# Two rows of a feed-forward input copied within SBUF and transposed as rounded 32-bit, and a final norm whose sum of squares goes straight into the power

## The chip, the cores and the metric

The kernel runs on one core of one Trainium2 chip. The core has five engines that work side by side and wait for each other by semaphores: TensorE (PE, with its weight loads listed as PEld), VectorE (DVE), ScalarE (ACT), GpSimd (POOL) and SyncE (SP), which here only issues transfers (DMAs). Data live in SBUF (128 partitions) and matmul results in PSUM. The metric is the device time of one execution in microseconds. Three executions before the change took 1324.27, 1325.01 and 1326.56 us; their median, 1325.01, is the time before.

## The reference

One decoder block on a sequence of 1024 tokens with a model width of 1024, in 32-bit floating point. What matters here is its second half and the last norm:

```python
def rmsnorm(x, g):
    xf = x.astype(jnp.float32)
    xf = xf * lax.rsqrt(jnp.mean(xf * xf, axis=-1, keepdims=True) + EPS)
    return (xf * g.astype(jnp.float32)).astype(x.dtype)

h = rmsnorm(x, mix_norm_g[l])
...
x = x + y @ w_out[l]
h = rmsnorm(x, ffn_norm_g[l])
x = x + (jax.nn.silu(h @ w_gate[l]) * (h @ w_up[l])) @ w_down[l]
...
return rmsnorm(x, final_norm_g)
```

Ahead of it two attention mixers (a sliding window with sinks and a latent one) are computed from `h`, gated and summed to `y`.

## The kernel before, in words

The 1024 tokens are worked on as eight blocks of 128 rows. Every product of two 32-bit matrices is made of three matmuls (`mm3`, L172 to L174): each operand is split into a rounded part and a remainder (`split`, L163 on ACT and L166 on DVE), in a rounded 32-bit type ("fp32r" in the profile), and high by high, high by low and low by high are added in PSUM. The large products (output projection, gate and up, down) are done as a 2 x 2 block product with seven instead of eight block products, numbered q = 1 to 7; the sums of blocks that this needs are formed on DVE and POOL.

**The way into the feed-forward part.** While the last products of the output projection (`xo`, PSUM tiles `xo`) end, each block b of the residual `x2[b]` goes through these steps. `norm_a(b)` squares it on ACT with a running sum (L1742) and forms the reciprocal root on POOL (`rstd_of`, L361 and L364). `norm_b(b)` multiplies it on DVE by that root and by the gain, into the tile `xn` (L1747), and sends the residual to DRAM (L1748, `x_d<-x` in the profile). `to_h_of(b)` calls `to_h(xn, b)`: eight transposes of 128 x 128 on PE by an identity matrix (L1583), four into each of two PSUM tiles `tp`, which ACT and DVE then take out. For b = 0 to 3 they are split at once. For b = 4 to 7 the block sums with block b − 4 are formed too (tiles `t`, `hraw`, then `t2h`, `t2l`, `t3h`, `t3l`, `b22h`, `b22l`); the second part of this, `rest()` (L1611 and the two lines after), is called later as `lowers.pop(b)()`. From there the feed-forward products run as `ffn.run()`, PSUM tiles `fa` and `fb`.

**What sets the order.** Here the order on PE, DVE, ACT and POOL is that of the program text (`manual_schedule` on these four); SP's queue is ordered by the scheduler, except where `keep_in_program_order` pins a transfer. An engine works its queue strictly in order, so a wait holds back all that is behind it. SBUF tiles come from two shared pools of slots, `U` (21 slots) and `V` (17). A tile gets the slot of one that is finished, and its first writer waits for the last users of that one. One tile more changes which slots the next ones get.

**The end.** The down projection runs q by q over eleven pairs of tiles (`lr`, split to `lrv`; PSUM tiles `fd`). `down_done(q, t)` is called for each of four row tiles t when a product is complete; it adds the product to the residual quarter `xq[(i, d)]` (i the half of the rows, d the half of the columns) and squares that quarter on ACT with a running sum into `fin_s` (`sumsq`, L1931). For the first quarter of a row the sum is scaled and the gain multiplied in at once (`first_half`, L1948 and L1950); for the second quarter `final` (L1936 to L1943) adds the two sums, raises to the power −1/2 on POOL, and scales both quarters, one on DVE and one on ACT, which are sent out. In the last product, q = 3, the last five pairs are done row tile by row tile, so that three of the four row tiles are finished beside matmuls.

Of the kernel before, what the change touches and what calls it, by code (L numbers as in the profile page):

```python
# [8 lines left out]
F32 = mybir.dt.float32  # L9
F32R = mybir.dt.float32r  # L10
BF16 = mybir.dt.bfloat16
AF = mybir.ActivationFunctionType
ALU = mybir.AluOpType
# [4 lines left out]
P = 128  # L18
S = 1024
D = 1024  # L20
NB = S // P
NK = D // P
EPS = 1e-6
# [66 lines left out]
def hybrid_block_kernel(  # L90
# [29 lines left out]
    nc = tc.nc  # L120
# [19 lines left out]
    def uid(name):  # L140
        counter[0] += 1
        return f"{name}_{counter[0]}"

    def U(name, dt=F32, shape=(P, 1024)):
        return pool.tile(list(shape), dt, tag="u", name=uid(name))

    def V(name, dt=F32, shape=(P, 4, 512)):
        return vpool.tile(list(shape), dt, tag="v", name=uid(name))

    def tiny(name, w=1):  # L150
        return small.tile([P, w], F32, tag=f"t{w}", name=uid(name))

    def P1(name, shape=(P, 512), dt=F32):
        return ps1.tile(list(shape), dt, tag="ps", name=uid(name))

    def PX(name, shape=(P, 512), dt=F32):
        return psum["x"].tile(list(shape), dt, tag="ps", name=uid(name))
# [18 lines left out]
    def sub(out, a, b, eng):  # L176
        eng.tensor_tensor(out, a, b, op=ALU.subtract)  # L177

    def add(out, a, b, eng):
        eng.tensor_tensor(out, a, b, op=ALU.add)  # L180

    def blk(b, n=1):
        return slice(b * P, (b + n) * P)

    def half(s):
        return slice(512 * s, 512 * s + 512)


    ident_r = const.tile([P, P], F32R, name="ident_r")
    ident = ident_r.bitcast(F32)  # L190
# [168 lines left out]
    def rstd_of(ss, width, r=None):  # L359
        ms = tiny("ms")  # L360
        nc.gpsimd.tensor_scalar(ms, ss, 1.0 / width, EPS, op0=ALU.mult, op1=ALU.add)  # L361
        if r is None:
            r = tiny("rstd")
        nc.gpsimd.tensor_tensor(r, ms, neg_half, op=ALU.pow)  # L364
        return r

    def bcast_gain(name, g, w=1024):
        t = U(name)
        nc.sync.dma_start(t[:, 0:w], g.partition_broadcast(P))
        return t  # L370
# [57 lines left out]
    for g in range(NG):  # L428
        t = V("khd", F32R, (P, 2, S))
# [141 lines left out]
    ps = kvq_ps[0] = PX("kvq")  # L571
# [122 lines left out]
    def new_h(name):  # L694
        hq[name] = (V(name + "h", F32R), V(name + "l", F32R))

    def split_h(name, c, src, eng=None):
        hi, lo = hq[name]
        split(hi[:, :, blk(c)], lo[:, :, blk(c)], src, eng)
# [60 lines left out]
    ORDER = (1, 6, 2, 7, 5, 4, 3)  # L760
# [155 lines left out]
    for b in range(NB):  # L916
# [4 lines left out]
        ps = PX("ql", (P, 416))  # L921
# [12 lines left out]
        t = U("lat", F32, (P, C_CKV))  # L934
# [102 lines left out]
    for i, b in enumerate((4, 5, 6, 7, 0, 1, 2, 3)):  # L1037
        ps = P1("kl", (P, KVL))
        mm3(ps, [(hT(k, blk(b)), (wkl[k // 4][0][:, k % 4], wkl[k // 4][1][:, k % 4])) for k in range(NK)])
        t = U("lat", F32, (P, 2, KVL))  # L1040
# [3 lines left out]
        r = rstd_of(ss, KVL)  # L1044
# [531 lines left out]
    def to_h(xn, b):  # L1576

        c = b % 4
        pss = []
        for kh in range(2):  # L1580
            ps = (P1 if b < 5 else PX)("tp", (P, 4, P))
            for j in range(4):
                nc.tensor.transpose(ps[:, j], xn[:, blk(4 * kh + j)], ident)  # L1583
            pss.append(ps)
        if b < 4:
            if b == 0:
                new_h("b11")
                new_h("b21")
            raw1[b] = U("hraw", F32, (P, 2, 4, P))
            for kh in range(2):  # L1590
                nc.scalar.copy(raw1[b][:, kh], pss[kh])
                split_h(("b11", "b21")[kh], c, pss[kh])
            return
        if b == 4:
            for name in ("b22", "t2", "t3"):
                new_h(name)
        r = raw1.pop(c)
        t23 = U("t23", F32, (P, 2, 4, P))
        nc.scalar.copy(t23[:, 1], pss[0])
        sub(r[:, 0], pss[0], r[:, 0], nc.vector)  # L1600
        b22, t2, t3 = ([t[:, :, blk(c)] for t in hq[name]] for name in ("b22", "t2", "t3"))
        nc.scalar.copy(b22[0], pss[1])
        sub(t23[:, 0], pss[1], r[:, 0], nc.vector)
        nc.scalar.copy(t2[0], t23[:, 0])
        sub(t23[:, 1], pss[1], t23[:, 1], nc.vector)
        sub(b22[1], pss[1], b22[0].bitcast(F32), nc.vector)
        sub(r[:, 1], r[:, 1], t23[:, 0], nc.gpsimd)
        late.append((c, r))

        def rest():  # L1610
            nc.scalar.copy(t3[0], t23[:, 1])  # L1611
            sub(t2[1], t23[:, 0], t2[0].bitcast(F32), nc.vector)
            sub(t3[1], t23[:, 1], t3[0].bitcast(F32), nc.vector)

        return rest
# [103 lines left out]
    normed = {}  # L1719
# [16 lines left out]

    wop = {}

    def norm_a(b):
        xn = U("xn")  # L1740
        ss = tiny("ss")
        nc.scalar.activation(xn, x2[b], AF.Square, accum_out=ss)  # L1742
        normed[b] = xn, rstd_of(ss, D)

    def norm_b(b):
        xn, rs = normed[b]
        nc.vector.scalar_tensor_tensor(xn, x2[b], rs, fg_bc, op0=ALU.mult, op1=ALU.mult)  # L1747
        nc.sync.dma_start(x2_d[b], x2.pop(b))  # L1748

    def to_h_of(b):  # L1750
# [67 lines left out]
    xo(3, 0)  # L1818
    conv(7, 1)
    norm_a(0)  # L1820
    ahead(4, 1)
    ffn.load_part(0, 1)
    xo(6, 2)
    conv(4, 0)
    norm_b(0)
    xo(3, 1)
    conv(4, 1)
    norm_a(1)
    mix_of("g")
    nc.scalar.activation(tiny("si"), neg_half, AF.Silu)  # L1830
    xo(6, 3)
    norm_b(1)
    to_h_of(0)
    xo(3, 2)
    norm_a(2)
    mix_of("u")
    ffn.prep_to(2)
    xo(7, 0)
    norm_b(2)
    to_h_of(1)  # L1840
    xo(3, 3)
# [62 lines left out]
    while ffn.n_run < len(ffn.seq):  # L1904
        j, q, m = ffn.run()
# [13 lines left out]
    xq = {}  # L1919
# [4 lines left out]

    p1, u2, u3 = V("dp1"), V("du2"), V("du3")
    fing = bcast_gain("fing", fin_g)
    fin_s = const.tile([P, 2, 2, 4], F32, name="fin_s")

    def sumsq(i, d, t):
        junk = U("sq", F32, (P, 512))  # L1930
        nc.scalar.activation(junk, xq[(i, d)][:, t], AF.Square, accum_out=fin_s[:, i, d, t:t + 1])  # L1931

    def final(i, t, d):

        fs = fin_s[:, i, d, t:t + 1]
        nc.gpsimd.tensor_scalar(fs, fs, 1.0 / D, fin_s[:, i, 1 - d, t:t + 1], op0=ALU.mult, op1=ALU.add)  # L1936
        nc.gpsimd.tensor_tensor(fs, fs, neg_half, op=ALU.pow)
        y = xq[(i, d)][:, t]
        nc.vector.scalar_tensor_tensor(y, y, fs, fing[:, half(d)], op0=ALU.mult, op1=ALU.mult)
        nc.sync.dma_start(out[blk(4 * i + t), half(d)], y)  # L1940
        y = xq[(i, 1 - d)][:, t]
        nc.scalar.mul(y, y, fs)
        nc.scalar.dma_start(out[blk(4 * i + t), half(1 - d)], y)  # L1943

    def first_half(i, t, d):

        fs = fin_s[:, i, d, t:t + 1]
        nc.gpsimd.tensor_scalar(fs, fs, 1.0 / D, EPS, op0=ALU.mult, op1=ALU.add)  # L1948
        y = xq[(i, d)][:, t]
        nc.gpsimd.tensor_tensor(y, y, fing[:, half(d)], op=ALU.mult)  # L1950

# [2 lines left out]
    def down_done(q, t):  # L1954
        ps = banks["A" if q in (1, 2, 5, 3) else "B"][t]
        if q == 1:
            nc.scalar.copy(p1[:, t], ps)
        elif q == 6:
            add(u2[:, t], ps, p1[:, t], nc.vector)
            add(u2[:, t], u2[:, t], xq[(0, 1)][:, t], nc.gpsimd)  # L1960
        elif q == 7:
            add(u3[:, t], ps, p1[:, t], nc.vector)
            add(u3[:, t], u3[:, t], xq[(1, 1)][:, t], nc.gpsimd)
            add(p1[:, t], p1[:, t], xq[(1, 0)][:, t], nc.gpsimd)
        else:
            i, d = {2: (0, 0), 5: (1, 1), 4: (1, 0), 3: (0, 1)}[q]
            x_ = xq[(i, d)][:, t]
            add(x_, ps, {2: x_, 5: u3[:, t], 4: p1[:, t], 3: u2[:, t]}[q], nc.vector)
            sumsq(i, d, t)
            if q in (4, 3):  # L1970
                final(i, t, d)
            else:
                first_half(i, t, d)

    i = 0
    for q in ORDER:
# [12 lines left out]
        if not last_q:  # L1989
            for j in range(HF):  # L1990
                down_ahead(i)
                if i in (8, 14, 20, 26):
                    load_x2(*((0, 1), (0, 0), (1, 1), (1, 0))[(i - 8) // 6])
                for t in range(4):
                    step(j, t)
                lr.pop((q, j))
                i += 1
            for t in range(4):
                down_done(q, t)
        else:  # L2000
            for j in range(HF - LAST):
                down_ahead(i, HF, CONVS + 1)
                for t in range(4):
                    step(j, t)
                i += 1
            down_ahead(i, HF, HF)
            for t in range(4):
                for j in range(HF - LAST, HF):
                    step(j, t)
                down_done(q, t)  # L2010
# [90 lines left out]
```

## Time and profile before

| what | value |
|---|---|
| median of three runs | 1325.01 us (1324.27 to 1326.56) |
| profiled execution: its own time | 1323.36 us |
| profiled execution: its span, first to last instruction | 1320.8 us |
| TensorE busy in the span | 1308.5 us (99%) |
| VectorE busy | 916.1 us (69%) |
| ScalarE busy | 635.7 us (48%) |
| GpSimd busy | 560.8 us (42%) |
| granted TensorE clock, mean | 0.998 of full |
| moved by DMA | 245.12 MB |

The span is 2.6 us shorter than the execution's own time. A row of the timeline gives start and length in microseconds, the engine, the line of the kernel, the operation, output and inputs by the program's names, the shape, and in brackets how long the engine sat idle before it and what ended that. Matmuls overlap: one of 512 columns is listed with 0.39 us, but they start 0.23 us apart. "SPq" is SP's queue: the time shown there is that of issuing a transfer, not of its landing. A row of a stage gives the stage's bounds and length, the busy time of PE, PEld, DVE, ACT and POOL, the granted clock, the share of the DMA engines and GB/s.

### The profile page before, as it was taken

What the parts mean: (1) busy time and instruction counts of PE and PEld (TensorE: products, weight loads), DVE (VectorE), ACT (ScalarE), POOL (GpSimd) and SP (SyncE); (2) the same over time, 40 slices, a digit from 0 to 9 for tenths busy, and PEclk for the clock granted to TensorE, in tenths of its full rate; (3) what the DMA queues carried; (4) which work ended last, traced back from release to release, by engine and by line L of the source; (5) the groups of instructions that cost most, each with busy time, mean ns of one, the idle gap of its engine ahead of it and who ended that gap; (6) DMA issues with size and microseconds to landing.
All of it is one profiled execution on the core that took longest, in us unless ns stands there. A gap on an engine that the chain in (4) does not pass through costs nothing.

```text
span 1320.8 us, 19066 instructions
## 1 busy us (share of the span) xinstructions
PE 1308.5 (99%) x6516; PEld 1102.8 (83%) x6516; DVE 916.1 (69%) x1509; ACT 635.7 (48%) x1289; POOL 560.8 (42%) x623
## 2 busy tenths in 40 slices
PE   9999999999999999999999999999999999999997
PEld 6899888888888888888888888888888888888886
DVE  7868687786767777877779655756666554663962
ACT  7434667675456666654455232332223323644452
POOL 2115546552325556312232465777567631022521
PEclk9999999999999999999999999999999999999999
DMA  9454444456576478898521334655554435996503
GB/s 375 161 187 160 133 161 138 154 177 215 164 250 181 104 216 192 266 306 199 185 112 48 124 135 162 233 201 197 184 183 148 147 120 197 373 375 226 175 20 140
DMA packets 92192, 245.12 MB, mean 186 GB/s; under 512 B 10304, under 2 KB 17984, under 8 KB 90944
## 3 DMA queue, kind: packets, MB, share of 16 engines
q1 hardware_dynamic: 87264, 233.15, 51.0%
q0 software_dynamic: 3392, 8.39, 3.6%
q10 hardware_dynamic: 1440, 2.36, 0.5%
q8 instruction: 52, 0.85, 0.3%
q14 instruction: 44, 0.36, 0.1%
HBM read 161.16 MB, written 78.51 MB: 181 GB/s over the span
## 4 chain that ended last, share of the span: by engine, by line
PE 60%; POOL 2%; issue 2%; DVE 2%; ACT 1%; DMA 0%; POOLq 0%; DVEq 0%; SPq 0%; ACTq 0%
PE fa L172 6%; PE fa L174 6%; PE fa L173 6%; PE fd L173 5%; PE fd L174 5%; PE fd L172 5%; PE fb L173 5%; PE fb L174 5%; PE fb L172 5%; PE xo L174 2%; PE xo L173 2%; PE xo L172 2%; POOL p L1266 1%; POOL denb L1265 1%; PE oB L174 1%
## 5 line engine op out<-in xcount | busy, mean ns | idle before, releaser
L166 DVE TENSOR_TENSOR wl<-wr,wl 128x512 fp32r<-128x512 f32 x150 | 144.3, 986 | 74.0 <-ACT wl L163 73.5
L166 DVE TENSOR_TENSOR lrv<-lr,lrv 128x1024 fp32r<-128x1024 f32 x77 | 105.2, 1397 | 49.4 <-ACT lrv L163 43.4
L163 ACT CAST lrv<-lr 128x1024 fp32r<-128x1024 f32 x77 | 80.1, 1052 | 94.1 <-PE fd L174 52.2
L172 PE MATMUL fd<-lrv 128*128 128x512 f32 x308 | 119.8, 389 | 0.0
L173 PE MATMUL fd<-lrv 128*128 128x512 f32 x308 | 119.8, 389 | 0.0
L174 PE MATMUL fd<-lrv 128*128 128x512 f32 x308 | 119.8, 389 | 0.0
L177 POOL TENSOR_TENSOR wr<-wr,sm 128x512 f32<-128x512 f32 (+1 forms) x38 | 45.6, 1209 | 137.9 <-DVE wl L166 119.6
L163 ACT CAST wl<-wr 128x512 fp32r<-128x512 f32 x150 | 86.5, 621 | 3.8 <-DVE t3l L177 2.8
L166 DVE TENSOR_TENSOR wl<-sm,wl 128x512 fp32r<-128x512 f32 x60 | 50.3, 862 | 42.8 <-ACT wl L163 42.6
L1265 POOL TENSOR_TENSOR denb<-denb,neg_one 128x1 f32<-128x1 f32 x64 | 39.9, 623 | 92.6 <-ACT p L1264 80.7
L172 PEld LDWEIGHTS fd<-lrv 128*128 128x128 f32 x308 | 57.8, 188 | 12.1
L173 PEld LDWEIGHTS fd<-lrv 128*128 128x128 f32 x308 | 57.8, 188 | 12.0
L174 PEld LDWEIGHTS fd<-lrv 128*128 128x128 f32 x308 | 57.8, 188 | 11.9
L1264 ACT ACTIVATE p<-scb,nmb 128x384 f32<-128x384 f32 (+3 forms) x64 | 47.7, 746 | 32.0 <-DVE nmb L1263 24.9
L361 POOL TENSOR_SCALAR ms<-ss 128x1 f32<-128x1 f32 x32 | 8.6, 269 | 122.8 <-ACT xn L1742 45.5
L1263 DVE CUSTOM_DVE_ANT_0 scb<-scb,mask 128x384 f32<-128x384 f32 (+3 forms) x64 | 48.4, 761 | 17.4 <-PE scb L1255 16.4
L1638 ACT ACTIVATE act<-sm 128x512 f32<-128x512 f32 x11 | 7.0, 633 | 102.2 <-DVE sm L180 102.2
L166 DVE TENSOR_TENSOR ptl<-pTb,pth 128x512 fp32r<-128x512 f32 (+2 forms) x96 | 50.0, 550 | 8.0 <-ACT pth L163 7.8
L163 ACT CAST pth<-pTb 128x512 fp32r<-128x512 f32 (+2 forms) x96 | 43.4, 480 | 18.2 <-PE pTb L1280 17.2
L1266 POOL TENSOR_SCALAR p<-p,denb 128x384 f32<-128x384 f32 (+3 forms) x64 | 48.4, 756 | 6.3
L1638 ACT ACTIVATE act<-pu 128x512 f32<-128x512 f32 x22 | 13.9, 632 | 69.7 <-DVE pu L180 69.7
L172 PE MATMUL fa<-t1h,wl 128*128 128x512 f32 x120 | 47.1, 392 | 0.1
(354 smaller groups left out, 4291.0 us busy)
## 6 DMA issues: line engine op xcount, KB each, us to landing
lr<-la_d SPq DMA_DIRECT2D x77, 256.0 KB, 5.3
wr<-in_w_gate_dram SPq DMA_DIRECT2D x22, 512.0 KB, 4.4
wr<-in_w_up_dram SPq DMA_DIRECT2D x22, 512.0 KB, 5.1
la_d<-sd SPq DMA_DIRECT2D x22, 512.0 KB, 4.9
wd<-in_w_down_dram SPq DMA_DIRECT2D x22, 512.0 KB, 7.0
rb_d<-wd SPq DMA_DIRECT2D x22, 512.0 KB, 2.7
lr<-rb_d SPq DMA_DIRECT2D x44, 256.0 KB, 5.4
lr<-in_w_down_dram SPq DMA_DIRECT2D x33, 256.0 KB, 5.3
```

Source lines behind the costliest of these rows:

```text
L163: i = nc.scalar.copy(hi, src)
L166: (eng or nc.vector).tensor_tensor(lo, src, hi.bitcast(F32), op=ALU.subtract)
L172: nc.tensor.matmul(ps, ah, bh, start=first and i == 0, stop=False, skip_group_check=go_on)
L173: nc.tensor.matmul(ps, ah, bl, start=False, stop=False, skip_group_check=go_on)
L174: nc.tensor.matmul(ps, al, bh, start=False, stop=last and i == n - 1, skip_group_check=go_on)
L177: eng.tensor_tensor(out, a, b, op=ALU.subtract)
L361: nc.gpsimd.tensor_scalar(ms, ss, 1.0 / width, EPS, op0=ALU.mult, op1=ALU.add)
L1263: nc.vector.tensor_tensor_reduce(s_, s_, m_, 1.0, -NEG, op0=ALU.add, op1=ALU.min, accum_out=nm)
L1264: nc.scalar.activation(p_, s_, AF.Exp, scale=-1.0, bias=nm, accum_out=den)
L1265: nc.gpsimd.tensor_tensor(den, den, neg_one[:, 0:1], op=ALU.pow)
L1266: nc.gpsimd.tensor_scalar(p[:, 0:w], p[:, 0:w], den, 0.0, op0=ALU.mult, op1=ALU.add)
L1638: nc.scalar.activation(dst, src, AF.Silu)
```

## The change

Three things are edited.

1. For blocks 6 and 7, `norm_b` sends `xn` by a transfer on SP's queue into a new tile `xr` of the rounded 32-bit type (the bytes stay as they are), and the transposes read `xr` with the identity in that type, into PSUM tiles of that type.
2. The sum of squares of the last product's quarter is formed on DVE (`sumsq_v`), by one instruction that multiplies, adds up and starts from the sum of the other quarter. The addition of the two sums on POOL is then not needed for these four row tiles. For the other four it stays, as an addition alone.
3. The factor 1/D is taken out of the sums: the constant becomes D times EPS, and the gain is multiplied once by the root of D, on ACT.

```diff
@@ to_h
-            ps = (P1 if b < 5 else PX)("tp", (P, 4, P))
+            r = b in RAW_T
+            ps = (P1 if b < 5 else PX)("tp", (P, 4, P), F32R if r else F32)
             for j in range(4):
-                nc.tensor.transpose(ps[:, j], xn[:, blk(4 * kh + j)], ident)
-            pss.append(ps)
+                nc.tensor.transpose(ps[:, j], xn[:, blk(4 * kh + j)], ident_r if r else ident)
+            pss.append(ps.bitcast(F32) if r else ps)
@@ ahead of norm_a
+    RAW_T = (6, 7)
@@ norm_b
         nc.vector.scalar_tensor_tensor(xn, x2[b], rs, fg_bc, op0=ALU.mult, op1=ALU.mult)
+        if b in RAW_T:
+            xr = U("xr", F32R)
+            tc.keep_in_program_order(nc.sync.dma_start(xr.bitcast(F32), xn))
+            normed[b] = xr, rs
         nc.sync.dma_start(x2_d[b], x2.pop(b))
@@ final norm
     fing = bcast_gain("fing", fin_g)
+    nc.scalar.mul(fing, fing, D ** 0.5)
...
+    def sumsq_v(i, d, t):
+        junk = U("sq", F32, (P, 512))
+        y = xq[(i, d)][:, t]
+        nc.vector.tensor_tensor_reduce(junk, y, y, 1.0, fin_s[:, i, 1 - d, t:t + 1], op0=ALU.mult, op1=ALU.add,
+                                       accum_out=fin_s[:, i, d, t:t + 1])
...
-        nc.gpsimd.tensor_scalar(fs, fs, 1.0 / D, fin_s[:, i, 1 - d, t:t + 1], op0=ALU.mult, op1=ALU.add)
+        if (i, d) == (1, 0):
+            nc.gpsimd.tensor_tensor(fs, fs, fin_s[:, i, 1 - d, t:t + 1], op=ALU.add)
         nc.gpsimd.tensor_tensor(fs, fs, neg_half, op=ALU.pow)
...
-        nc.gpsimd.tensor_scalar(fs, fs, 1.0 / D, EPS, op0=ALU.mult, op1=ALU.add)
+        nc.gpsimd.tensor_scalar(fs, fs, 1.0, D * EPS, op0=ALU.mult, op1=ALU.add)
...
-            sumsq(i, d, t)
+            if q == ORDER[-1]:
+                sumsq_v(i, d, t)
+            else:
+                sumsq(i, d, t)
```

On SP's queue, at the last residual stores (`x_d<-x`; `x_7150` is block 6, `x_7152` block 7), this stood before; the names in brackets are the semaphores that the row waits for (DMAHW: an earlier transfer):

```order
L1748 DMA x_d<-x_7150 128x1024 [waits DMAHW1_49,DVE_49]
L1748 DMA x_d<-x_7152 128x1024 [waits DMAHW2_49,DVE_49]
L1627 DMA wr_7718<-in_w_gate_dram 128x1024 [waits DMAHW3_49,PE_49,Activation_49]
L1627 DMA wr_7718<-in_w_up_dram 128x1024 [waits DMAHW4_49]
L1656 DMA la_d_93<-act_7809 128x512 [waits DMAHW5_49,DVE_49]
```

And this stands now, where `xn_7661` is the normalized block 6 and `xn_7706` block 7:

```order
L1755 DMA x_d<-x_7150 128x1024 [waits DMAHW1_49,DVE_49]
L1755 DMA x_d<-x_7152 128x1024 [waits DMAHW2_49,DVE_49]
L1753 DMA xr_7714<-xn_7661 128x1024 [waits DMAHW1_49,DMAHW3_49,DVE_49,Activation_49]
L1628 DMA wr_7720<-in_w_gate_dram 128x1024 [waits DMAHW4_49,PE_49]
L1628 DMA wr_7720<-in_w_up_dram 128x1024 [waits DMAHW5_49]
L1753 DMA xr_7758<-xn_7706 128x1024 [waits DMAHW6_49,DVE_49,PE_49]
L1657 DMA la_d_93<-act_7813 128x512 [waits DMAHW7_49,DVE_49]
```

The copy of block 6 stands behind the store of block 7 and ahead of the two loads of weight tiles, the copy of block 7 behind them; DMAHW1 at the first copy is the store of block 6, whose slot `xr` takes.

On ACT, from the last cast of block 4 to the one of block 6, this stood before (`tp_7736` and `tp_7775` are the first PSUM tiles of blocks 5 and 6):

```order
L1611 CAST t3h_7682<-t_1446_7684 128x4x128
L864 COPY pu_7734<-fa_7721 128x512 [waits DMAHW1_49,DVE_49,Activation_49]
L1599 COPY t_1456_7746<-tp_7736 128x512 [waits PE_49]
L1602 CAST b22h_7678<-tp_7741 128x4x128
L1604 CAST t2h_7680<-t_1456_7746 128x4x128 [waits DVE_49]
L163 CAST wl_7757<-wr_7575 128x512 [waits DMAHW5_49,Activation_49,Pool_49]
L864 COPY pu_7773<-fa_7760 128x512 [waits PE_49]
L1599 COPY t_1462_7785<-tp_7775 128x512 [waits PE_49]
```

And this stands now, in the same order (`tp_7738` and `tp_7779` are those PSUM tiles):

```order
L1612 CAST t3h_7682<-t_1446_7684 128x4x128
L864 COPY pu_7736<-fa_7723 128x512 [waits PE_49]
L1600 COPY t_1457_7748<-tp_7738 128x512 [waits DVE_49,Pool_49]
L1603 CAST b22h_7678<-tp_7743 128x4x128
L1605 CAST t2h_7680<-t_1457_7748 128x4x128 [waits DVE_49]
L163 CAST wl_7761<-wr_7575 128x512 [waits DMAHW5_49,DMAHW3_49]
L864 COPY pu_7777<-fa_7764 128x512 [waits DMAHW1_49,PE_49]
L1600 COPY t_1464_7789<-tp_7779 128x512 [waits DMAHW2_49,DVE_49]
```

Nothing has moved, but the slots have: the copy of block 5 out of PSUM waits for DVE (its `t3l` of block 4) and POOL, the cast `wl` for the landing of the copy of block 6 (DMAHW3), and the copy of block 6 out of PSUM for DVE (the normalization of block 7) and for that block's store (DMAHW2).

On PE the transposes keep their place; between the last matmul ahead and the first behind stand now the rows of block 6, the first of which waits for its copy's landing:

```order
L174 MATMUL fa_7764<-b11h_7424,wl_7462 128x512
L1584 MATMUL tp_7779<-ident_r,xr_7714 128x128 [waits DMAHW3_49,DVE_49]
L1584 MATMUL tp_7779<-ident_r,xr_7714 128x128 x3
L1584 MATMUL tp_7784<-ident_r,xr_7714 128x128 [waits DVE_49]
L1584 MATMUL tp_7784<-ident_r,xr_7714 128x128 x3
L172 MATMUL fa_7723<-b21h_7426,wl_7517 128x512 [waits Activation_49]
```

Before, the first of them waited for DVE alone, that is for the normalization itself:

```order
L174 MATMUL fa_7760<-b11h_7424,wl_7462 128x512
L1583 MATMUL tp_7775<-ident_r,xn_7661 128x128 [waits DVE_49]
L1583 MATMUL tp_7775<-ident_r,xn_7661 128x128 x3
L1583 MATMUL tp_7780<-ident_r,xn_7661 128x128 x4
L172 MATMUL fa_7721<-b21h_7426,wl_7517 128x512 [waits Activation_49]
```

So a transfer stands now between DVE and PE where a semaphore stood. At the end of the program DVE has, for each of the four row tiles of the last product, two instructions more between the addition and the scaling (the square with its sum, and the reading of the accumulator), ACT one fewer (the square), and POOL goes from two instructions to the power alone.

## The prediction

> **What bounds the kernel now.** I read the engine table of the page first, then TensorE (PE) stage by stage, then the timeline around the two places that the change touches, 680 to 707 us and the last 7 us.
>
> ```profile
> PE 1308.5 (99%) x6516; PEld 1102.8 (83%) x6516; DVE 916.1 (69%) x1509; ACT 635.7 (48%) x1289; POOL 560.8 (42%) x623
> 690.00:707.20 17.20, 17.15 (x80) 13.71 (x78) 16.95 (x24) 11.14 (x21) 7.30 (x5) 1.00 0.13 47
> 707.20:1313.80 606.60, 606.52 (x2675) 501.88 (x2675) 375.55 (x420) 212.55 (x329) 280.61 (x204) 1.00 0.51 182
> ```
>
> The second and third lines are stages: length, then busy time of PE, PEld, DVE, ACT and POOL, the granted clock, the DMA share and GB/s. From 707 us to the last matmul PE is without work for 0.08 of 606.60 us. So whatever delays PE near 690 us reaches the end of the program undiminished, except for two short waits that PE has in 690 to 707 us. There DVE is as full as PE (16.95 of 17.20 us), so a shift on DVE counts too.
>
> This is the timeline of that place. Block 6 is normalized by DVE (L1747 at 685.92) and transposed by PE (L1583, weight loads from 688.10); block 7 is at 691.41 and 697.36.
>
> ```profile
> 685.92 1.28 DVE L1747 SCALAR_TENSOR_TENSOR xn<-x,rstd,ffng 128x1024 f32<-128x1024 f32 x1
> 686.03 0.32 SPq L1748 DMA_DIRECT2D x_d<-x  x1
> 686.45 0.37 SPq L1627 DMA_DIRECT2D wr<-in_w_gate_dram  x1
> 687.81 0.69 DVE L177 TENSOR_TENSOR t3l<-t,t3h 128x512 fp32r<-128x512 f32 x1
> 688.09 0.39 PE L174 MATMUL fa<-b11h,wl 128*128 128x512 f32 x1
> 688.10 1.02 PEld L1583 LDWEIGHTS tp<-ident_r,xn 128*128 128x128 f32 x8
> 688.16 0.59 ACT L1599 COPY t<-tp 128x512 f32<-128x512 f32 x1
> 688.32 1.04 PE L1583 MATMUL tp<-ident_r,xn 128*128 128x128 f32 x8
> 689.12 0.48 PE L172 MATMUL fa<-b21h,wl 128*128 128x512 f32 x1
> 691.41 1.35 DVE L1747 SCALAR_TENSOR_TENSOR xn<-x,rstd,ffng 128x1024 f32<-128x1024 f32 x1
> 691.85 0.59 ACT L1599 COPY t<-tp 128x512 f32<-128x512 f32 x1
> 692.01 0.19 PEld L172 LDWEIGHTS fa<-b21h,wl 128*128 128x128 f32 x1 [0.32 <-ACT pu L864]
> 697.36 1.03 PEld L1583 LDWEIGHTS tp<-ident_r,xn 128*128 128x128 f32 x8
> 698.03 0.59 ACT L864 COPY pu<-fa 128x512 f32<-128x512 f32 x1
> 699.64 0.68 DVE L177 TENSOR_TENSOR hraw<-tp,hraw 128x512 f32<-128x512 f32 x1
> 707.09 0.19 PEld L173 LDWEIGHTS fb<-t2l,wl 128*128 128x128 f32 x1 [0.47 <-DVE t2l L177]
> ```
>
> Between the end of the normalization of block 6 (685.92 + 1.28 = 687.20) and PE's use of it lie 0.90 us; for block 7 it is 697.36 − 692.76 = 4.60 us. The brackets at 692.01 and 707.09 are PE's two waits, 0.32 and 0.47 us.
>
> **The change part by part.** *The copies.* Each sends 512 KB from one SBUF tile to another, through SP's queue. Before, the attention probabilities go the same way in the same size, `per<-pe`:
>
> ```profile
> L1095 SPq DMA_DIRECT2D per<-pe x16: 470/471/738, 143.6 to 306.3; - x16
> DMA to landing us min/median/max: 2.7/3.1/4.9
> ...
> L1095 SPq DMA_DIRECT2D per<-pe x1: 470/470/470, 165.1 to 165.1; - x1
> DMA to landing us min/median/max: 3.2/3.2/3.2
> ```
>
> The one at 165.1 us is followed half a microsecond later by a weight load, as the copy of block 6 will be, so I take its 3.2 us; 2.7 and 4.9 us are the ends. SP has sent the store of block 7's residual at 686.03 and is then free, so it issues the copy when DVE is done, at 687.23 (the store at 686.03 shows how little lies between), and it lands at 690.43. PE wanted to load weights at 688.10 and now stands until 690.43, **2.33 us** (1.83 to 4.03). Everything queued on PE behind the transposes waits with them. On SP the two loads of weight tiles behind the copy go out about 1.3 us later than 686.45; their first reader on ACT is some 8 us away, and a copy in the queue costs them nothing that shows. The copy of block 7 goes out at about 693.2 and lands at 696.4, before the 699 us at which the delayed PE asks for it: nothing.
>
> *The transposes.* The same shape with 32-bit rounded type on both sides is in the trace at L1118:
>
> ```profile
> 328.66 0.39 PE L174 MATMUL fb<-t3h,wl 128*128 128x512 f32 x1
> 328.89 0.81 PE L1118 MATMUL lT<-ident_r,lat 128*128 128x128 f32 x8
> 329.55 0.46 PE L172 MATMUL fa<-t1h,wl 128*128 128x512 f32 x1
> ```
>
> From the end of the matmul ahead to the end of the one behind: 330.01 − 329.05 = 0.96 us, against 689.60 − 688.48 = 1.12 us for block 6. That is 0.16 us a block, **−0.32 us** for both (0 if the typing does nothing, −0.4 at most).
>
> *Slots.* The copies take two more tiles from the shared pool, and the tiles that come after them get other slots. By the order, ACT's copy of block 5 out of PSUM (688.16) now waits for DVE's t3l (ends 688.50), and that of block 6 (691.85) for the normalization of block 7. The first shifts DVE by about 0.35 us, so block 7 is normalized until 693.15; ACT then starts on block 6 at about 693.2 instead of 691.85, and DVE is about 0.5 us late. Both lie beside the stalled PE. ACT's pu copy at 698.03 then waits for the late matmuls: they end about 1.8 us later, it starts at 699.7, the transposed block 7 is taken up 1.2 us later than 699.64, and DVE's t2l, for which PE waits at 707.09, is 1.2 us late. PE comes there 2.33 − 0.16 − 0.17 − 0.16 = 1.84 us late (0.17 is what the wait at 692.01 cost the stream of matmuls, about half of its 0.32; it is gone, since ACT is done before PE arrives). So PE no longer waits at 707.09 either: about 0.4 us of the 0.47 come back. PE leaves this place 1.84 − 0.43 = **+1.41 us** late.
>
> *The final gain* is scaled once on ACT, 128x1024:
>
> ```profile
> L369 SPq DMA_DIRECT2D fing<-in_fin_g_dram x1: 333/333/333, 1102.6 to 1102.6; - x1
> ...
> 1117.68 1.05 ACT L163 CAST lrv<-lr 128x1024 fp32r<-128x1024 f32 x1 [13.41 <-DMA lr<-in_w_down_dram]
> ```
>
> A 128x1024 pass takes 1.05 us, and it stands in front of this cast, in 13.41 us in which ACT waits for a load: nothing. If that cover were gone, the cast would be at most 1.05 us late.
>
> *The tail.* After the last matmul of a row tile comes this chain (first six lines), and the last one ends the program. The last two lines are the only fused multiply-and-reduce of that width on DVE:
>
> ```profile
> 1313.76 0.69 DVE L180 TENSOR_TENSOR xq<-fd,du 128x512 f32<-128x512 f32 x1 [0.16 <-PE fd L174]
> 1314.48 0.63 ACT L1931 ACTIVATE sq<-xq 128x512 f32<-128x512 f32 x1 [0.91 <-DVE xq L180]
> 1315.02 0.19 ACT L1931 ACTIVATION_READ_ACCUMULATOR sq<-xq 128x1 f32 x1
> 1315.31 0.27 POOL L1936 TENSOR_SCALAR fin_s<-fin_s 128x1 f32<-128x1 f32 x1 [2.50 <-ACT sq L1931]
> 1315.66 0.55 POOL L1937 TENSOR_TENSOR fin_s<-fin_s,neg_half 128x1 f32<-128x1 f32 x1
> 1316.24 0.75 DVE L1939 SCALAR_TENSOR_TENSOR xq<-xq,fin_s,fing 128x512 f32<-128x512 f32 x1 [1.79 <-POOL fin_s L1937]
> ...
> 402.43 0.70 DVE L1263 CUSTOM_DVE_ANT_0 scb<-scb,mask 128x512 f32<-128x512 f32 x1 [0.50 <-PE scb L1255]
> 403.05 0.14 DVE L1263 DVE_READ_ACCUMULATOR2_ANT nmb<- 128x1 f32 x1
> ```
>
> The new square on DVE reads what the add has just written and waits for its end (1314.45), about 0.1 us more; 0.62 us later the accumulator is read for 0.14 us, until 1315.3; 0.1 us to POOL as from ACT at 1315.31, and the power starts at 1315.4 instead of 1315.66. **−0.2 us** (−0.4 if the square follows the add at once, +0.1 if it is slower from SBUF). For the three row tiles before, this is beside matmuls: DVE has 0.69 + 0.76 + 0.75 us of work in the 3.4 us that PE takes for one.
>
> **Sum.** 1.41 − 0.2 = +1.2 us. The profiled execution has a span of 1320.8 us and a time of 1323.36, so 1322.0 and 1324.6 are expected of one like it; it lay 1.65 us under the median of the runs, 1325.01, which becomes **1326.2 us**. About 0.2%, 2.65 us, is what a measurement tells from no change, so the likeliest result is "same".
>
> **The rivals.** *TensorE falls to half its clock in the gap.* PE would stand from 688.48 to 690.43, about 2 us. The end of the program shows what a quiet PE leads to:
>
> ```profile
> 1313.72:1315.91 2.19, 0.00 (x1) 0.00 (x0) 0.69 (x1) 0.72 (x2) 0.52 (x2) 1.00 0.63 239
> 1315.91:1320.80 4.89, 0.00 (x0) 0.00 (x0) 0.75 (x1) 0.72 (x1) 0.30 (x1) 0.50 0.28 107
> ...
> 1.24 3.59 PE L562 MATMUL warm<-warm 128*128 128x512 bf16 x8 [1.24 <-DVE warm L559]
> ```
>
> After 2.19 us without a matmul the granted clock goes from 1.00 to 0.50. At the start, eight matmuls of 512 columns take 3.59 us, 0.45 each, where the stream later has one each 0.23: half rate for about 3.6 us, which would cost 1.8 us here. That gives +3.0 us, 1328.0, slower. It decides if the copy lands a little later than I take it, or if the gap lies badly to whatever samples the activity. The page "TensorE: Matmul & The Clock Gate" of the Trainium skill (section "What's actually happening") says that the clock halves after at least one idle window of about 3.4 us; by that rule a gap of 2 us leaves it alone and the sum stands. The rows above, with a drop after 2.19 us, do not bear out so long a time, so I keep the rival.
>
> *The copy is slow*, 4.9 us as the slowest of the sixteen: PE stands 1.7 us longer, ACT's next cast waits for the same landing, and the gap of 3.6 us makes the half clock likely: +2.9 to +4.7, 1328 to 1330. For it speaks that two transfers are near it in the queue; against it that fifteen of sixteen were faster.
>
> *The copy is hidden anyway*: it would have to land 0.9 us after its issue, and no copy did in under 2.7. If PE did not stand, DVE's 0.5 us from the slots would still reach PE at 707.09, and with the tail's −0.2 it would be +0.3, 1325.3.
>
> *The typing doesn't make transposes faster*: 0.32 us come back, 1326.5.
>
> **How the numbers follow.** The sum as worked out has 0.62, the half clock 0.17, the slow copy 0.06, the hidden copy 0.05, the useless typing 0.07; 0.03 is for what I don't see. Only the half clock and the slow copy come over +2.65 us: slower 0.22. Faster by that much would need more than all the savings together (0.9 us): 0.03. Same 0.75. The range goes from the shortest copy with the larger tail (+0.5, less 1.2 us for the spread of the runs, 1324.3) to the half clock with a little of the slow copy (1328.7).
>
> **What will show it.** PE's wait in front of the transposes of block 6, released by the copy's landing, near 2.3 us; eight transposes in about 0.73 us; no waits at 692 and 707 us; POOL's power 0.2 us sooner after the last matmul; PE busy without a gap from there to the last matmul. The forecast is wrong if PE doesn't wait for the copy, if the granted clock shows 0.5 behind the gap, or if the shifted slots bring a wait of PE after 707 us.

## The result, and the profile after

The changed kernel takes 1326.54 us (median of 20 executions, 1324.77 to 1328.56); the kernel before, run beside it, 1325.03 us (20 executions, 1322.73 to 1326.91). The ratio on record is 1.0016 with a 95% interval of 1.0010 to 1.0022: 2.1 us slower (1.3 to 2.9), while the two medians lie 1.5 us apart. The interval of the loss holds no zero, so there is one; at 0.16% it is less than the 0.2% that the prediction took as the border of "same". The profiled execution took 1327.82 us with a span of 1325.7 us.

In this execution everything ahead of the change is already 2.07 us later than in the profile of before (block 5's transposes start at 686.78 instead of 684.71 us). So I measure the change by a stretch of its own, called the **path** below: from the start of block 5's transposes to the end of the last matmul. It took 1313.72 − 684.71 = 629.01 us before and 1318.57 − 686.78 = 631.79 us after, 2.78 us more.

The timeline of the changed kernel around block 6 (L1750 normalizes, L1753 sends the copy, L1584 transposes):

```profile
687.77 1.28 DVE L1750 SCALAR_TENSOR_TENSOR xn<-x,rstd,ffng 128x1024 f32<-128x1024 f32 x1
689.12 0.52 SPq L1753 DMA_DIRECT2D xr<-xn  x1
690.45 0.59 ACT L1600 COPY t<-tp 128x512 f32<-128x512 f32 x1 [0.33 <-DVE t3l L177]
692.56 1.23 PE L1584 MATMUL tp<-ident_r,xr 128*128 128x128 f32 x8 [2.01 <-DMA xr<-xn]
702.94 0.80 PE L1584 MATMUL tp<-ident_r,xr 128*128 128x128 f32 x8
```

PE is idle for 2.01 us, and the copy's landing ends that, as forecast. ACT's copy of block 5 waits 0.33 us for `t3l`, as the slots said. From the tile's view, the landings of the two copies:

```profile
L1753 SPq DMA_DIRECT2D xr<-xn x2: 513/518/524, 689.1 to 695.1; - x2
...
DMA to landing us min/median/max: 2.9/3.1/3.3
```

PE's waits from 685 to 720 us, all of them (time in all, times, longest), first PE, then its weight loads; those that stood at 692 and 707 us before are gone:

```profile
PE tp L1584 <- DMA xr<-xn: 2.0, 1, 2.0
...
PEld tp L1584 <- DVE hraw L177: 2.4, 1, 2.4
```

The weight loads wait for the same copy: `hraw` was done at 691.07 + 0.69 = 691.76 us, and they start at 692.53, just behind the landing.

And the stages of that place:

```profile
689.10:692.52 3.42, 1.45 (x7) 0.87 (x5) 2.56 (x5) 2.09 (x5) 1.47 (x2) 1.00 0.91 320
692.52:695.93 3.41, 3.37 (x14) 2.92 (x15) 3.36 (x6) 2.58 (x5) 1.30 (x1) 0.50 0.66 246
695.93:707.00 11.07, 11.07 (x55) 9.20 (x54) 8.67 (x15) 6.27 (x13) 2.43 (x2) 1.00 0.18 73
712.00:1318.60 606.60, 606.57 (x2677) 502.08 (x2675) 377.04 (x425) 211.73 (x324) 280.95 (x201) 1.00 0.51 182
```

The clock (third number from the right) is granted at 0.50 for 3.41 us behind the gap: PE gets 14 instructions done where a full clock allows 20, as behind the same wait in the profile of e10 (below):

```profile
693.80:697.20 3.40, 3.39 (x20) 2.94 (x21) 3.34 (x6) 2.39 (x5) 1.30 (x1) 1.00 0.65 247
```

That is the rival of the half clock, and it happened. Afterwards PE has no gap up to the last matmul. The tail:

```profile
1318.61 0.69 DVE L180 TENSOR_TENSOR xq<-fd,du 128x512 f32<-128x512 f32 x1 [0.50 <-PE fd L174]
1319.34 0.75 DVE L1944 CUSTOM_DVE_ANT_0 sq<-xq,fin_s 128x512 f32<-128x512 f32 x1
1320.01 0.08 DVE L1944 DVE_READ_ACCUMULATOR2_ANT fin_s<- 128x1 f32 x1
1320.17 0.55 POOL L1952 TENSOR_TENSOR fin_s<-fin_s,neg_half 128x1 f32<-128x1 f32 x1 [2.85 <-DVE fin_s L1944]
```

From the addition's start to the power's start it is 1320.17 − 1318.61 = 1.56 us, before 1315.66 − 1313.76 = 1.90: 0.34 us shorter. The gain reaches the last store, which SP issues 2.97 us behind the end of the last matmul (1321.54 − 1318.57) where it was 3.30 (1317.02 − 1313.72). The span of these two profiles doesn't show it: they end 7.0 and 7.1 us behind the last matmul, and between all profiles that stretch varies by more than the gain (6.7 to 7.2 us with the new tail, 7.0 and 7.4 with the old).

### The profile page after: what moved, and what is told of

Same layout as the page of the kernel before. It is cut to its first block, busy times and chain, and to the rows that moved or that the text cites. A ratio compares the mean times of both kernels' runs of the same rounds, so it can differ in the third digit from the quotient of the medians.

```text
span 1325.7 us, 19071 instructions
## 1 busy us (share of the span) xinstructions
PE 1311.3 (99%) x6516; PEld 1104.8 (83%) x6516; DVE 919.0 (69%) x1517; ACT 634.8 (48%) x1282; POOL 560.9 (42%) x619
## 4 chain that ended last, share of the span: by engine, by line
PE 61%; issue 2%; POOL 2%; DVE 2%; ACT 1%; DMA 0%; POOLq 0%; DVEq 0%; ACTq 0%
PE fa L172 6%; PE fa L173 6%; PE fa L174 6%; PE fd L172 5%; PE fd L173 5%; PE fd L174 5%; PE fb L174 5%; PE fb L173 5%; PE fb L172 5%; PE xo L172 2%; PE xo L173 2%; PE xo L174 2%; PE pTb L1280 1%; PE oB L173 1%; PE oB L172 1%
## 5 line engine op out<-in xcount | busy, mean ns | idle before, releaser
L172 PE MATMUL fb<-t2h,wl 128*128 128x512 f32 x120 | 47.0, 392 | 0.0
```

The lines of the kernel that those rows point to most:

```text
L172: nc.tensor.matmul(ps, ah, bh, start=first and i == 0, stop=False, skip_group_check=go_on)
```

## The experiments

Theory: PE stands for the landing of block 6's copy, and in a part of the executions the clock halves behind that gap; the typing and the tail give a little back. Rivals: the wait alone is the loss; the shifted slots on DVE and ACT are; the tail is. Of each profile the table gives the path and its three parts: from block 5's transposes (b5) to those of block 6 (b6), to those of block 7 (b7), and to the last matmul, in us, each read as a difference of start times; then whether the clock fell to 0.5 there, and the ratio of the times to the kernel before.

| kernel | b5 to b6 | b6 to b7 | b7 to end | path | clock 0.5 | ratio (95%) |
|---|---|---|---|---|---|---|
| before | 3.61 | 9.26 | 616.13 | 629.01 | no | 1 |
| after | 5.78 | 10.38 | 615.63 | 631.79 | yes | 1.0016 (1.0010 to 1.0022) |
| e1 tail only | 3.61 | 9.07 | 615.95 | 628.63 | no | 0.9996 (0.9987 to 1.0005) |
| e2 copies only | 5.68 | 8.96 | 615.59 | 630.23 | no | 1.0016 (1.0007 to 1.0025) |
| e3 block 7 only | 3.61 | 9.07 | 616.14 | 628.82 | no | 1.0002 (0.9993 to 1.0011) |
| e4 nine matmuls in the gap | 5.71 | 8.89 | 615.65 | 630.25 | no | 1.0008 (0.9998 to 1.0019) |
| e5 copy sent twice | 10.22 | 11.58 | 615.60 | 637.40 | yes | 1.0066 (1.0053 to 1.0079) |
| e6 block 6 transposed later | 6.33 | 6.42 | 616.64 | 629.39 | no | 1.0005 (0.9997 to 1.0014) |
| e7 copy in two halves | 4.62 | 9.35 | 615.65 | 629.62 | no | 1.0006 (0.9997 to 1.0014) |
| e8 copies untyped | 5.47 | 9.11 | 615.77 | 630.35 | no | 1.0012 (1.0003 to 1.0020) |
| e9 after, again | 5.46 | 10.56 | 615.59 | 631.62 | yes | 1.0019 (1.0010 to 1.0028) |
| e10 three matmuls in the gap | 5.92 | 8.97 | 615.59 | 630.47 | no | 1.0021 (1.0012 to 1.0031) |

An interval is about ±1.2 us wide for the ten or eleven executions of a kernel here. The path is finer, but it is one execution each, and it too varies by some 0.4 us: e1 does not touch the place at all and has 0.38 us less than the kernel before, because PE's wait at 692 us is missing and that at 707 us is 0.27 instead of 0.47 us.

**e1, the tail alone.**

```diff
-    RAW_T = (6, 7)
+    RAW_T = ()
```

> The copies and the typing are undone (blocks 6 and 7 are transposed from the normalized tile as before); the final norm's new sum and the scaled gain are kept. My account (the loss is PE standing for the landing of block 6's copy, with a half clock behind it in part of the executions; the tail gains 0.3 us): no wait of PE ahead of block 6's transposes, no drop of the clock before the end, 1324.7 us, 0.3 under the kernel before. Rival (the tail is what costs, for instance DVE's square beside matmuls): 1326 or more, and a wait of PE after 707 us.

Median 1322.95 beside 1323.67 us. There is no wait of PE at block 6 and none behind it beyond that of 0.27 us; addition to power takes 1.57 us (1318.56 to 1320.13). So the tail does not cost anything that these times show. Its profile shows a thing that I had not looked for: early in the program, in a part that no edit touches, the clock halves too (last section).

**e2, the copies alone.** The final norm is put back to what it was.

```diff
-    nc.scalar.mul(fing, fing, D ** 0.5)
...
-            if q == ORDER[-1]:
-                sumsq_v(i, d, t)
-            else:
-                sumsq(i, d, t)
+            sumsq(i, d, t)
```

> The final norm is as before; both copies and the typed transposes are kept. My account: PE stands 2.2 us ahead of block 6's transposes, 1326.5 us without a drop of the clock and 1328.2 with it, so about 1327 over the executions, 2 us over the kernel before. Rival (the tail is what costs): within 0.5 us of the kernel before.

Median 1325.98 us, 2.3 us over the kernel before. With e1 beside it, the loss lies in the copies. This profile has the wait without the drop of the clock:

```profile
691.38 0.84 PE L1584 MATMUL tp<-ident_r,xr 128*128 128x128 f32 x8 [1.91 <-DMA xr<-xn]
```

```profile
686.88:690.29 3.41, 2.60 (x12) 1.81 (x10) 2.69 (x4) 3.08 (x6) 1.47 (x2) 1.00 0.75 288
690.29:693.70 3.41, 2.32 (x15) 2.09 (x16) 3.28 (x5) 1.71 (x4) 1.30 (x1) 1.00 0.92 328
```

The second fence is the stages view with two neighbouring stretches of 3.41 us that divide the gap; the clock stays at 1.00. The path is 1.22 us longer than before, against 1.41 forecast; in the changed kernel's profile, with the drop, it is 2.78 us.

**e3, block 7 alone.**

```diff
-    RAW_T = (6, 7)
+    RAW_T = (7,)
```

> Only block 7 is copied and transposed as rounded 32-bit; block 6 goes as before; the tail is as changed. My account: the copy of block 7 lands over a microsecond before PE asks for it, so no stall and no drop of the clock; the transposes of block 7 are 0.16 us faster, of which PE's wait at 707 us may swallow all; the tail gives 0.3: 1324.5 to 1324.8 us. Rival (the shifted slots on DVE and ACT cost by themselves): a longer wait of PE near 699 or 707 us and 1325.5 or more.

Median 1324.18 beside 1323.67 us, with an interval that holds zero. PE does not wait for this copy: the transposes stand without a bracket.

```profile
698.30 0.79 PE L1584 MATMUL tp<-ident_r,xr 128*128 128x128 f32 x8
```

```profile
707.81 0.19 PEld L173 LDWEIGHTS fb<-t2l,wl 128*128 128x128 f32 x1 [0.68 <-DVE t2l L177]
```

What the faster transposes save is waited away at 707 us, where PE now stands for DVE 0.68 us. A gain on PE alone is worth nothing at this place.

**e4 and e10, matmuls in the gap.** Nine, or three, matmuls of 512 columns are added ahead of block 6's transposes; their result is overwritten by these.

```diff
+            if b == 6 and kh == 0:
+                for _ in range(FILL):
+                    nc.tensor.matmul(ps.bitcast(F32).rearrange("p a c -> p (a c)"), ident_r, hq["b11"][0][:, 0],
+                                     start=True, stop=True)
```

> The changed kernel with nine matmuls of 512 columns added ahead of block 6's transposes, into the PSUM tile that these overwrite. They wait for nothing and take the place of PE's idle time (9 x 0.23 = 2.1 us), so the path still waits for the copy, but PE isn't quiet for more than about 0.3 us. If the half clock behind the gap is a part of the loss: no granted clock of 0.5 before the end in any execution, and a mean about 0.8 us under the changed kernel's, near 1325.8 (the changed kernel without the executions at 1327 and more). If the clock's drop doesn't matter and the wait alone is the loss: as the changed kernel, 1326.5. If the added matmuls last longer than the wait, up to 0.3 us more.

> The changed kernel with three matmuls of 512 columns ahead of block 6's transposes (their result is overwritten), so that PE is quiet for about 1.3 us instead of 2.0 while the path waits as long. Theory: no stretch of the grid can hold 1.95 us of idle time, so the clock never drops there; block 5's transposes to the last matmul take 630.2 us, and the median lies under that of the changed kernel on this chip by about 0.8 us (1.6 us in about half of the executions). Rival (the clock behind the gap makes nothing of the loss): the same median and spread as the changed kernel.

By the profiles both are as the theory has it: the wait stays on the path (b5 to b6 5.71 and 5.92 us), the clock does not fall, and the path is 630.25 and 630.47 us, 1.2 to 1.5 us under the two profiles of the changed kernel. By the times only e4 agrees: its median is 1.4 us over the kernel before, with an interval of the ratio that still overlaps that of the changed kernel. e10's median, 1327.04 us, is no better than that of the changed kernel on the same chip (1326.79, e9). That expectation missed. In the profiled e10, 1327.46 us, block 5 came at 687.89 us, 3.18 us later than in the profile of before; whether its other executions come as late is not shown, so the cause stays open.

How often the clock falls can be read from another number. The executions of these kernels each have a mean granted clock on record, to three places, and a stretch of 3.41 us at half speed takes 1.71 of some 1325 us off it, that is 0.0013. In the kernels with a wait for a whole copy (after, e2, e8, e9) 21 of 53 executions have 0.997, as the two profiles with the drop have. In the kernel before it is 1 of 82, in e1, e3, e6 and e7 together 1 of 44, and with matmuls in the gap (e4, e10) 2 of 21. So the drop comes in about four of ten executions, and matmuls in the gap mostly keep it away. Of the 31 executions of the changed kernel (after, e9) the 15 with 0.997 have a median of 1327.2 us, the other 16 one of 1325.7: the difference, 1.5 us, is about the price that the profiles show. The mean does not tell where in the program the clock fell, so the count is rough.

**e5, the copy of block 6 sent twice.**

```diff
-            tc.keep_in_program_order(nc.sync.dma_start(xr.bitcast(F32), xn))
+            for _ in range(2 if b == 6 else 1):
+                tc.keep_in_program_order(nc.sync.dma_start(xr.bitcast(F32), xn))
```

> The copy of block 6 is sent twice, one after the other, so that the wait of PE ahead of block 6's transposes grows by one more landing, about 3.2 us, to a quiet of some 5.2 us. Theory (a stretch of the clock's grid of 3.41 us in which PE is idle for about 1.95 us or more halves the granted clock for the next one): the drop now comes in every execution, whatever the phase, and costs about 1.6 us (0.9 to 2.4) on top of the wait: about 6 us over the kernel before (1.2 wait as it is, 3.2 more, 1.6 clock), and a granted clock of 0.5 behind the gap in the profile. Rival (the drop comes with the gap but costs nothing that the path sees): 4.4 over the kernel before, and matmuls behind the gap at the usual 0.23 us.

Median 1331.93 us, 8.0 us over the kernel before (1323.89): more than either theory. The wait grew by 4.5 us, since the second copy landed only after 4.7 us. All six executions have a mean granted clock of 0.995 or 0.996, where the kernel before, run beside it, has 0.998 or 0.999, so the clock fell in each of them, as expected. In the profile it stayed at half for three stretches:

```profile
688.67:692.09 3.42, 1.36 (x7) 0.78 (x5) 2.56 (x5) 1.99 (x5) 1.44 (x3) 1.00 0.92 326
692.09:695.50 3.41, 0.00 (x0) 0.00 (x0) 2.73 (x4) 1.50 (x3) 1.09 (x1) 0.50 0.92 357
695.50:698.91 3.41, 2.43 (x11) 2.17 (x12) 1.10 (x3) 1.09 (x2) 0.00 (x0) 0.50 0.37 150
698.91:702.33 3.42, 3.42 (x10) 2.64 (x9) 2.93 (x5) 1.14 (x2) 1.29 (x1) 0.50 0.01 2
702.33:712.00 9.67, 9.67 (x49) 8.03 (x48) 5.11 (x9) 4.92 (x10) 1.06 (x1) 1.00 0.08 29
```

The stretch from 695.50, with PE busy for 2.43 of 3.41 us, did not bring the full clock back here; the next one, with PE busy throughout, did. From b6 to b7 it takes 11.58 us, 2.62 more than in e2. So the wait and the half clock both reach the end, and the rival in which the half clock costs nothing is out: it would have left 8.96 there.

**e6, block 6 transposed later.** The transposes are put behind the next call of the feed-forward products.

```diff
     ffn.prep_to(6)
     ffn.run()
-    to_h_of(6)
     ffn.prep_to(7)
     ffn.run()
+    to_h_of(6)
     lowers.pop(5)()
```

> The changed kernel with block 6's transposes moved behind the next four-by-three matmuls of the feed-forward part, 2.7 us later in PE's queue. Theory (the loss is the exposed landing alone): the copy has landed by then, PE doesn't wait, no drop of the clock before the end; of the faster transposes (0.16 us a block, two blocks) something stays, and the tail's 0.3: 0.3 to 0.6 us under the kernel before, from block 5's transposes to the last matmul 628.3 to 628.8 us against 629.0. Rival (the shifted slots and DVE, which is full there, carry the delay anyway): PE waits at the place where it waited at 707 us, by 0.5 us or more, and the time is that of the kernel before or more.

The copy is hidden, and still the path is 0.38 us longer than before instead of 0.2 to 0.7 shorter; the median is 1324.15 beside 1323.89 us. The rival has it. Three waits of PE stand in the timeline in the place of one:

```profile
694.21 0.19 PEld L172 LDWEIGHTS fa<-b21h,wl 128*128 128x128 f32 x1 [0.19 <-ACT pu L864]
706.06 0.19 PEld L172 LDWEIGHTS fa<-b21h,wl 128*128 128x128 f32 x1 [0.35 <-ACT pu L864]
709.80 0.19 PEld L173 LDWEIGHTS fb<-t2l,wl 128*128 128x128 f32 x1 [0.92 <-DVE t2l L177]
```

Between 680 and 710 us PE is not the only bound: DVE's chain from the transposed block to `t2l` is as tight. Time that PE does not spend waiting for the copy is then waited for DVE. The edit has a part in this itself: it brings block 6's transposes 6.33 us behind block 5's, later than the wait does (5.68 in e2), so DVE gets block 6 later too. What a copy hidden without moving the transposes would bring is not shown.

**e7, each copy in two halves by columns.**

```diff
-            tc.keep_in_program_order(nc.sync.dma_start(xr.bitcast(F32), xn))
+            for d in range(2):
+                tc.keep_in_program_order(nc.sync.dma_start(xr[:, half(d)].bitcast(F32), xn[:, half(d)]))
```

> Each copy is sent as two transfers of half the columns (256 KB each), so that the first four transposes wait for the first alone. If the landing grows with the size: the first half lands about 0.5 us earlier, PE is quiet for some 1.4 to 1.7 us, too short for a drop of the clock, and the loss to the kernel before is 0.5 to 0.9 us. If the landing is nearly all fixed time: the first half lands as late as the whole copy did, the second 0.5 us after it, and the loss is as in the changed kernel or 0.3 us more.

A landing grows with the size: 256 KB took 2.3 to 2.5 us, 512 KB 2.9 to 3.3.

```profile
DMA to landing us min/median/max: 2.3/2.4/2.5
```

```profile
692.33 0.51 PE L1584 MATMUL tp<-ident_r,xr 128*128 128x128 f32 x4 [0.85 <-DMA xr<-xn]
693.06 0.51 PE L1584 MATMUL tp<-ident_r,xr 128*128 128x128 f32 x4 [0.21 <-DMA xr<-xn]
```

PE waits twice, 0.85 and 0.21 us, instead of 2.0, less than expected; the path is 629.62 us, 0.61 over before, and with the tail's 0.34 about 0.3 us of loss are left, where 0.5 to 0.9 were expected. The times (0.75 us between the medians, −0.4 to 1.9 by the interval) agree, but can't tell this from no change.

**e8, copies and transposes in plain 32-bit.**

```diff
-            r = b in RAW_T
+            r = False
...
-            xr = U("xr", F32R)
-            tc.keep_in_program_order(nc.sync.dma_start(xr.bitcast(F32), xn))
+            xr = U("xr")
+            tc.keep_in_program_order(nc.sync.dma_start(xr, xn))
```

> Both copies are kept, but in plain 32-bit, and the transposes too. If the typing makes eight transposes 0.16 us faster: they take 1.03 us again, and the time from block 6's transposes to the last matmul is about 0.3 us longer than in the changed kernel without a drop of the clock (624.5), that is 624.85; the wait for the landing stays at about 2 us. If the typing does nothing: 624.5.

From b6 to the end it takes 9.11 + 615.77 = 624.88 us, in e2 8.96 + 615.59 = 624.55: the typing is worth 0.33 us. The other kernels with the typing and no drop agree with e2 to 0.01 us (624.54 in e4, 624.56 in e10). Block 7's transposes, in e8 and then in e2:

```profile
702.01 1.03 PE L1584 MATMUL tp<-ident_r,xr 128*128 128x128 f32 x8
```

```profile
700.35 0.80 PE L1584 MATMUL tp<-ident_r,xr 128*128 128x128 f32 x8
```

**e9, the changed kernel again.** No edit.

> The changed kernel once more, beside the next one on the same chip. Theory: PE is quiet for 1.9 to 2.2 us ahead of block 6's transposes; the granted clock drops behind it only if one stretch of the grid of 3.41 us (counted from the first event of the clock in that profile) holds 1.95 us or more of it, and then the stretch from block 5's transposes to the last matmul takes 631.8 us, otherwise 630.2. Over the executions some are 1.6 us slower than the others, and the median is about 1.5 to 2.1 us over the kernel before.

Median 1326.79 beside 1323.72 us, 2.5 us over by the ratio (1.3 to 3.7). The path is 631.62 us, with a drop, though the stretch ahead of it holds only 3.41 − 1.72 = 1.69 us of quiet, less than the 1.95 that I had set, so that limit was too high:

```profile
689.92:693.33 3.41, 1.72 (x13) 1.26 (x12) 2.57 (x5) 1.98 (x5) 1.51 (x2) 1.00 0.93 327
693.33:696.74 3.41, 3.41 (x9) 2.66 (x8) 3.15 (x5) 1.82 (x4) 0.46 (x1) 0.50 0.53 214
```

None of these versions beats the kernel before by more than a measurement tells; the tail alone comes nearest, with 0.9996.

## Why the prediction was right, and where it was not

The time, 1326.54 us against 1326.2, lies in the range and in the class "same". That it came so near is in part luck: the sum had the lasting delay a little too large and left out the half clock, and the two errors cancel. By its steps:

- *The stall at block 6*, 2.33 us from a landing of 3.2: b5 to b6 grew by 2.17 us, and by 1.85 to 2.31 in the other kernels that keep the exposed whole copy (e2, e4, e8, e9, e10). Right, and the landings of 2.9 to 3.3 us answer to the row that it was taken from.
- *The typing*, −0.32 us for both blocks: 0.33 in e8 against e2. Right.
- *What comes back behind it*: −0.16, −0.17, −0.16 and −0.43 make −0.92 us from b6 to the end. Without a drop it was 624.55 − 625.39 = −0.84 us (e2 against before). Right; both waits were gone, and ACT and DVE were late as the slots said. The size hangs on the profile that it is compared with: in e1, with nothing changed at this place, the same stretch took 625.02 us, which leaves −0.47.
- *PE leaves the place 1.41 us late*: 1.22, 1.24 and 1.46 us in e2, e4 and e10, which have no drop of the clock (1.60 to 1.84 against e1). Right within what one profile tells.
- *The tail*, −0.2 us: −0.34, within its ends. The step "the new square ... reads what the add has just written and waits for its end ... about 0.1 us more" was right in kind, but reading the accumulator took 0.08 and not 0.14 us, and POOL's power started 1.56 us after the addition's start where I had 1315.4 − 1313.76 = 1.64.
- *The copy of block 7, the gain scaled on ACT, the weight loads behind the copy*, each for nothing: the transposes of block 7 wait for nothing in any of the profiles that copy it, and PE has 0.03 us without work from 712 us on.
- *The half clock* is where the working failed. I had it as a rival with a chance of 0.17, which "decides if the copy lands a little later than I take it, or if the gap lies badly to whatever samples the activity". The second half of that sentence was the whole matter: it is no case against another, but a toss in each execution. Of the four profiles with the plain wait of 1.7 to 2.0 us two have the drop (after, e9) and two do not (e2, e8). By the mean granted clocks it fell in 21 of 53 executions. It should have stood in the sum, at about four tenths of its price. The prediction's own list of signs has it as one of being wrong "if the granted clock shows 0.5 behind the gap", and the profile of the changed kernel shows that. The price that I gave, 1.8 us, was 1.42 (10.38 − 8.96, after against e2) and 1.60 us (10.56 − 8.96, e9 against e2).
- *The hidden copy*, +0.3 us: e6 has 0.38 − 0.34 = 0.04 us by the profile. The wait for `t2l` that this rival names is there, 0.92 us at 709.80, but e6 moves the transposes as well. That the shifted slots alone lengthen this wait is seen better in e3, where block 6 is not copied: 0.68 us against 0.27 in e1.

With these sizes the changed kernel is 1.22 − 0.34 = 0.9 us slower without the drop and 2.78 − 0.34 = 2.4 us with it. With the drop in four of ten executions that makes about 1.5 us; the ratios, 2.1 (1.3 to 2.9) and 2.5 us (1.3 to 3.7), have it inside their intervals, and the medians lie 1.5 us apart at first and 3.1 in e9. What stays open is e10, whose times are longer than its path says.

## What to carry to other kernels

A transfer within SBUF that takes a semaphore's place costs its whole landing, here about 3 us for 512 KB, less whatever slack lay between producer and reader; ask for that slack first (0.90 us at block 6, 4.60 at block 7). Where two engines are equally full at a place, hiding the wait of one can just move it to the other, as in e6. A gap of some 2 us on TensorE, as here, is priced with the half clock that can follow it, as a term of the mean and not as a remote case; shortening the gap, as the two halves did, takes off both parts.

## What the runs showed of the hardware that I had not expected

**The clock falls on a grid, and half a stretch of quiet is enough.** In every profile the clock changes only at multiples of 3.413 us after its first change (in the kernel before 5.19 and 1315.91 us, 384 stretches apart; in e5 it stayed low for 10.24 us, three). These are stretches of that grid with the quiet of PE in them (length less busy time; the ends of matmuls are modelled, so by some 0.2 us), and the clock in the next one:

| profile and stretch, us | quiet, us | clock next |
|---|---|---|
| before, 1312.50 to 1315.91 | 2.19 | 0.5 |
| e5, 688.67 to 692.09 | 2.06 | 0.5 |
| e1, 152.75 to 156.17 | 2.05 | 0.5 |
| after, 1317.16 to 1320.57 | 2.00 | 0.5 |
| after, 689.10 to 692.52 | 1.97 | 0.5 |
| e3, 1312.94 to 1316.35 | 1.91 | 1.0 |
| e9, 689.92 to 693.33 | 1.69 | 0.5 |
| e1, 1316.70 to 1320.11 | 1.59 | 1.0 |
| e10, 692.66 to 696.08 | 1.15 | 1.0 |
| e2, 690.29 to 693.70 | 1.09 | 1.0 |

In these profiles the limit lies somewhere between 1.6 and 2.0 us, about half of a stretch; e3 and e9 stand in the wrong order, so it isn't sharper than that from the outside. A gap of 2 us thus halved the clock where it fell within one stretch (after, e9) and did not where it was divided between two (0.81 and 1.09 us in e2, 0.84 and 0.86 in e8). The page "TensorE: Matmul & The Clock Gate" of the Trainium skill (section "What's actually happening") says that the window of about 3.4 us runs freely, and the grid agrees; it gives one idle window as the condition for the low clock, and here 1.7 to 2.2 us of quiet in a window was enough.

**It strikes elsewhere, too.** In e1 PE waited 2.05 us for ACT at 155 us, in a part that is the same in all kernels, and the clock was at half for the next stretch:

```profile
155.26 0.50 PE L172 MATMUL fa<-t1h,wl 128*128 128x512 f32 x1 [2.05 <-ACT wl L163]
```

```profile
152.75:156.17 3.42, 1.37 (x9) 0.80 (x8) 0.93 (x2) 3.42 (x13) 1.22 (x2) 1.00 0.00 0
156.17:159.58 3.41, 3.41 (x9) 2.63 (x9) 2.99 (x6) 2.56 (x7) 3.32 (x6) 0.50 0.20 77
```

**The grid's phase at the start moves the whole program.** Where the clock's first rise came by 6.74 us (before, e2, e3, e4), block 5 was reached at 684.71 to 685.71 us; where it came at 9.37 to 10.66 us (all others), at 686.26 to 687.89 us, and in e1 at 689.89 with its drop at 156 us. The stages view shows the same matmuls at two rates in the same four microseconds, before and then after:

```profile
7.00:11.00 4.00, 4.00 (x10) 1.71 (x10) 3.51 (x9) 2.44 (x4) 0.00 (x0) 1.00 1.01 398
```

```profile
7.00:11.00 4.00, 4.00 (x7) 1.58 (x6) 3.36 (x8) 2.60 (x4) 0.00 (x0) 1.00 1.02 403
```

Ten instructions of PE, or seven, in a PE that is busy throughout. The later rise leaves 9.85 − 5.19 = 4.66 us more at half rate, which is 2.3 us of work; block 5 came 2.07 us later. The rise is not all: in e2 it came 0.98 us earlier than in before and block 5 still 1.00 us later, as PE waited longer for its first loads there (1.10 and 0.38 us for `wr`, 0.56 in before). (Ahead of the first change on record the clock column of this view shows 1.00 all the same.) A part of the 4 us by which executions of one kernel differ therefore seems to come from where on the grid the program happens to start, and a change of 1 to 2 us is better read from a stretch of the trace behind that point than from the times.
